# Half-size weight parts, a planner that counts the shared port of VectorE and GpSimd, packed sample rows, and values ahead of keys in a hybrid transformer step

## The chip, the cores and the metric

One core of a Trainium2 chip runs the whole program in one launch. The metric is the device time of that launch in microseconds (us). Engines are named as the profile names them: PE is TensorE (the weight loads ahead of its matmuls stand apart as PEld), DVE is VectorE, ACT is ScalarE, POOL is GpSimd, SP is SyncE, which issues nearly all DMAs.

## The reference, cut to what matters

One layer of a hybrid model, float32, for 256 prompt rows and 64 sample rows (8 requests of 8 rows). The layer has three parts side by side: sparse attention over keys that an indexer picks (A), a gated linear recurrence (B) and cross attention over a memory of 256 rows (M). Their gated outputs are joined, projected, added to the scaled input and normalized.

```python
z = jnp.einsum('btd,dn->btn', h, w)            # 2048 -> 8272 columns, 320 rows
aq, ak, av, ag, iq, ik, iw, bq, bf, bi, bg, mq, mg = jnp.split(z, cuts, axis=-1)
a_out = _dsa_prompt(aq, ak, av, iq, iw, ik)    # softmax over the top 64 keys of 256 (prompt)
...                                            # sample rows: top 256 of 2056, keys and values in cache pages
mk = jnp.einsum('bnd,dm->bnm', mem_prompt, w_mem_k[l])     # memory keys, 2048 -> 512, 256 rows
mv = jnp.einsum('bnd,dm->bnm', mem_prompt, w_mem_v[l])     # memory values, likewise
m_out = _mem_attend(mq, mk, mv)
...
cat = jnp.concatenate([a, b, m], axis=-1)
y = jnp.einsum('btn,nd->btd', cat, w_out)      # 2048 -> 2048
return _layernorm(ALPHA * h + y, ln_g, ln_b)   # rows of 2048
```

## The kernel before

**Weights.** All large products are made from two parts of each float32 operand, a rounded one (`wh`, `xh`) and the remainder (`wl`, `xl`), with three matmuls for each tile: `wh` by `xh`, `wh` by `xl`, `wl` by `xh`. Weights come in chunks of 128x1024 (512 KB) into a ring of three raw buffers `wr`. `prep` makes the parts of a chunk: ACT casts `wh<-wr`, then `wl<-wr,wh` is subtracted, on DVE for the first 52 chunks and after that (`TT`) on DVE or POOL, whichever the planner holds to be done first. `wh` and `wl` have two buffers of 128x1024 each. A raw buffer is free for the next load when its subtraction is done.

**Order.** Nothing is scheduled by the chip or a compiler: the order of each engine's instructions is what Python writes. Class `Plan` keeps a clock for each engine with estimated costs (`cost`) and latencies. The main loop of `hymba_step` goes by it: issue loads, `prep` up to one chunk ahead of the one that PE is at, evacuate finished accumulators (`pending`), let the generators of the side work go on (`background`: indexer, attention scores, softmax `soft`, recurrence `hgrn` and so on, by rank), then give PE either a unit of cached key or value pages (`unit`, `units_now`) or the next piece of a weight chunk (`pe_quantum`). Every instruction passes through one helper, so all rows have its line, L127 (L140 in the changed kernel). `T` chunks are the input projections (accumulated in `pj`), `mem` chunks the 16 of the memory keys and values (keys in two `mB` banks, values in two `pj` banks), `wo` chunks the output projection.

**A unit of pages** uses PE in another shape than the projections (`kv<-pg,qpad`, `va<-pg,PT`). `units_now` lets two follow each other, or one alone if PE has no weight piece ready.

**The output projection** runs in four column blocks n of 512; each has 8 chunks (two k tiles each), and for each chunk the row blocks m = 0, 1 (128 prompt rows each, accumulated in `mA` and `mB`, three matmuls for each k tile) and m = 2 (64 sample rows, `catS` as the weight of the array, two matmuls for each k tile, in `pj`). Of the last block, n = 3, the last `RES` = 5 chunks are kept: they are run for m = 0 alone, then all for m = 1, then all for m = 2, so that the first rows can be normalized while PE is still busy. Four of the kept chunks have their parts in memory that is spare by then (`cat0`, `cat1`, `PT`, one `pg`), the fifth in `wh` and `wl`.

**The end.** `out_chunk` adds ALPHA times the residual row to the accumulator and takes the statistics (`bn`); `finish(m)` normalizes: four pieces of 128x512, each with a DVE operation (subtract mean, times gain), an ACT scale and a POOL add of the bias. For the 64 sample rows (m = 2, in 64 of 128 partitions of a `pg` buffer) the first two pieces go that way and the other two have a second DVE operation instead of ACT and POOL. `ln_load` fetches the residual rows `xn` and the gain and bias (`lng`, `lnb`, 1 MB each).

## Time and profile before

| what | value |
|---|---|
| median of 3 runs | 922.3 us (920.91 to 923.38) |
| the profiled execution | 920.66 us |
| its span in the trace | 918.9 us, mean granted PE clock 0.991 |
| busy: PE, DVE, ACT, POOL | 884.9, 580.4, 384.6, 302.9 us |
| mean DMA rate over the span | 289 GB/s (265.53 MB) |

All rows of the trace come from the one profiled execution. It took 920.66 us, 1.76 more than its span and 1.64 less than the median. A window that shows less than its whole length as busy for PE holds waits; a wait row names the engine and the tile that ended the wait, which is the last of several that may have been late.

### The profile page before, as it was taken

The numbers are of one execution on the slowest core, as the hardware profiler recorded it, in microseconds if no ns is written. First come the engines' busy times: TensorE is split into PE (matmuls) and PEld (weight loads), VectorE is DVE, ScalarE is ACT, GpSimd is POOL, SyncE is SP. The second block draws the span as 40 slices with busy tenths as digits, with TensorE's granted clock in tenths as the row PEclk, the third lists the DMA queues.
The fourth block names the chain that finished last, engine by engine and source line by source line (L and its number), as shares of the span: only waits on it lengthen the run. The fifth ranks groups of instructions, "written<-read, shape, count | busy, mean of one in ns | idle before, by whom it ended". The sixth has DMA issues, their size and how long they took to land. (4 is left out here: it accounts for less than half of the span.)

```text
span 918.9 us, 18244 instructions
## 1 busy us (share of the span) xinstructions
PE 884.9 (96%) x6588; PEld 738.5 (80%) x6590; DVE 580.4 (63%) x1098; ACT 384.6 (42%) x677; POOL 302.9 (33%) x259
## 2 busy tenths in 40 slices
PE   8999999999999999999999999999899999999993
PEld 7999789868889987778878677778789788788872
DVE  6777995558999975757655653565354232645567
ACT  5334652544344344243443243434345232633342
POOL 0776858444644541332311311355100000011016
PEclk9999999999999999999999999999999999999997
DMA  8544435899999936999989889999994999744633
GB/s 300 176 169 151 142 100 195 334 325 359 396 367 352 386 140 220 409 383 382 367 320 401 335 304 401 404 393 337 367 336 144 409 406 381 244 144 148 202 115 114
DMA packets 79932, 265.53 MB, mean 289 GB/s; under 512 B 10081, under 2 KB 16930, under 8 KB 79266
## 3 DMA queue, kind: packets, MB, share of 16 engines
q1 hardware_dynamic: 77794, 260.17, 76.3%
q0 software_dynamic: 2048, 4.20, 1.4%
q8 instruction: 52, 0.85, 0.4%
q14 instruction: 38, 0.31, 0.1%
HBM read 255.60 MB, written 8.73 MB: 288 GB/s over the span
## 5 line engine op out<-in xcount | busy, mean ns | idle before, releaser
L127 PE MATMUL pj<-xh,wh 128*128 128x320 f32 x1008 | 324.7, 322 | 3.7 <-ACT t L127 3.7
L127 PE MATMUL pj<-xh,wl 128*128 128x320 f32 x1008 | 311.9, 309 | 1.2 <-POOL wl L127 1.1
L127 PE MATMUL pj<-xl,wh 128*128 128x320 f32 x1008 | 311.6, 309 | 0.0
L127 DVE TENSOR_TENSOR wl<-wr,wh 128x1024 fp32r<-128x1024 f32 x133 | 168.1, 1265 | 206.3 <-ACT wh L127 201.2
L127 ACT CAST wh<-wr 128x1024 fp32r<-128x1024 f32 x170 | 177.7, 1047 | 236.8 <-PE pj L127 196.1
L127 PEld LDWEIGHTS pj<-xh,wh 128*128 128x128 f32 x1008 | 189.8, 188 | 32.5 <-issue 23.5
L127 POOL TENSOR_TENSOR wl<-wr,wh 128x1024 fp32r<-128x1024 f32 x37 | 91.1, 2465 | 317.1 <-ACT wh L127 303.5
L127 PEld LDWEIGHTS pj<-xh,wl 128*128 128x128 f32 x1008 | 189.6, 188 | 1.8 <-POOL wl L127 1.3
L127 PEld LDWEIGHTS pj<-xl,wh 128*128 128x128 f32 x1008 | 190.1, 189 | 1.2
L127 POOL TENSOR_TENSOR t<-t,t 128x320 f32<-128x320 f32 (+4 forms) x74 | 68.1, 921 | 147.4 <-ACT t L127 88.9
L127 ACT ACTIVATE t<-t 128x320 f32<-128x320 f32 (+1 forms) x68 | 29.2, 454 | 77.0 <-DVE t L127 73.0
L127 PE MATMUL va<-pg,PT 128*32 128x512 f32 x512 | 60.6, 607 | 0.0
L127 PE MATMUL kv<-pg,qpad 128*32 128x256 f32 x1024 | 59.6, 381 | 0.0
L127 PEld LDWEIGHTS kv<-pg,qpad 128*32 128x32 f32 x1024 | 31.3, 110 | 23.0 <-issue 3.4
L127 POOL DMA_INDIRECT pg<-in_ci,poff x32 | 38.1, 1189 | 10.6 <-issue 8.2
L127 POOL DMA_INDIRECT S<-in_ci,poff x32 | 38.5, 1203 | 8.3 <-issue 6.6
L127 DVE MAX8 PT<-PT 128x8 f32<-128x1032 f32 x32 | 39.4, 1231 | 0.5
L127 DVE MATCH_REPLACE8 PT<-PT 128x1032 f32<-128x1032 f32 x32 | 39.0, 1218 | 0.0
L127 PEld LDWEIGHTS va<-pg,PT 128*32 128x32 f32 x512 | 14.6, 110 | 29.9 <-issue 27.2
L127 DVE TENSOR_TENSOR t<-t,t 128x128 f32<-128x128 f32 (+5 forms) x50 | 23.5, 472 | 21.0 <-ACT t L127 14.8
L127 PE MATMUL mB<-t,wh 128*128 128x256 f32 x128 | 25.8, 295 | 1.8 <-POOL t L127 1.7
L127 PE MATMUL mB<-t,t 128*128 128x64 f32 (+5 forms) x150 | 25.0, 314 | 2.2 <-POOL t L127 1.8
(309 smaller groups left out, 1280.5 us busy)
## 6 DMA issues: line engine op xcount, KB each, us to landing
pg<-in_ck SPq DMA_DIRECT2D x128, 512.0 KB
pg<-in_cv SPq DMA_DIRECT2D x128, 512.0 KB
...
```

The source lines that it names most:

```text
L127: res = f(*a, **k)
```

## The change

**Weight parts** are made in pieces of 512 columns. `prep(i, j)` casts and subtracts half a chunk; `wh` and `wl` have four buffers of 128x512; a piece of PE's work needs only its own half (`part_of`), and `prep` runs up to two chunks ahead. The 170 casts of 128x1024 become 338 of 128x512; the 133 subtractions on DVE become 246 and the 37 on POOL become 92, all of 128x512 (two small chunks at the start stay whole).

**The planner** knows a shared port: a DVE operation whose operands are all in SBUF is planned behind a POOL operation of that kind that is running. It adds 0.11 us where an operation reads what the one before it on its engine wrote, holds a change of PE's shape back to the full shape to be dearer (0.31 for 0.2), and lets a page unit run alone only if no weight piece will be ready within `SOON` = 0.4 us. `soft` gets the first rank in `background`, and waits (`need(maskb)`) before its last mask matmul.

**Prompt scores** are kept negated, so that the minimum serves as the bias of the exponential without a DVE negation; the two normalizing multiplies for each of 8 heads go from DVE to ACT.

**Memory chunks**: the values come first in the weight columns, each chunk has two pieces for PE (values, keys), and the value accumulators are evacuated (`mem_values`) apart from the keys (`mem_keys`).

**The output projection** keeps 7 chunks for n = 3 (five in spare memory), and the m = 2 pass runs in two column halves of 256, the first of which can be evacuated while the second runs.

**Sample rows** lie packed, 64 rows x 2 halves in 128 partitions of 1024 columns (`xs`, output `ys`), with a gain and bias laid out likewise (`gb`, 128x2x1024, 1 MB loaded in addition). `finish_sample` joins the statistics of the two halves by small copies between partitions and normalizes with four DVE operations of 128x512.

```diff
-RES = 5
+RES = 7
...
+        if eng != "PE" and t == self.t[eng] and not self.before[eng].isdisjoint(ki):
+            t += 0.11
+        if eng == "DVE" and port:
+            for a, b in self.port:
+                if a <= t < b - 0.1:
+                    t = b - 0.1
+        if eng == "POOL" and port:
+            self.port = self.port[-5:] + [(t, t + cost)]
+        self.before[eng] = set(ko)
...
-    for m in (1, 2):
+    for m, half in ((1, None), (2, 0), (2, 1)):
         for i in kept:
             add_wo(3, wspec[i]["k"], (m,), "main", ref=i)
+            wspec[-1]["half"] = half
...
+        w = s["n"] // s.get("parts", 2)
+        raw = WR[i][:, w * j:w * j + w]
+        if s.get("res") and kept.index(i) >= RES - 5:
             if not spare_w:
-                for cols, tag in ((2880, "cat0"), (2240, "cat1"), (2320, "PT"), (2048, "pg")):
+                for cols, tag in ((2880, "cat0"), (2240, "cat1"), (2320, "PT"), (2048, "pg"), (2048, "pg")):
                     t = new([128, cols], tag, F32R)
                     plan.split.add(t.tensor.name)
-                    spare_w.extend(t[:, 1024 * j:1024 * j + 1024] for j in range(t.shape[1] // 1024))
+                    spare_w.extend(t[:, 512 * k:512 * k + 512] for k in range(4))
             hi, lo = spare_w.pop(0), spare_w.pop(0)
...
-            hi, lo = new([128, 1024], "wh", F32R), new([128, 1024], "wl", F32R)
-        WH[i], WL[i] = whole[i] = hi, lo
-        ACT.copy(hi[:, 0:n], raw[:, 0:n])
+            hi, lo = new([128, 512], "wh", F32R), new([128, 512], "wl", F32R)
+            held["w"] += 1
+            s["held"] = True
+        WH[i].append(hi)
+        WL[i].append(lo)
+        ACT.copy(hi[:, 0:w], raw)
         if i < 52:
...
-        idle_pe = half >= len(wspec) or not half_ready(half, quarter)
-        return int(idle_pe and loaded(n) or plan.now > since[0] + PATIENCE)
+        return int(not half_soon() or plan.now > since[0] + PATIENCE)
...
-            DVE.tensor_tensor_reduce(out=P0, in0=ps[:, 0:128], in1=pbias[:, 0:128], scale=QS, scalar=FLOOR,
-                                     op0=OP.add, op1=OP.max, accum_out=s8[:, 0:1])
...
-            DVE.tensor_scalar(s8[:, 2:4], s8[:, 0:2], -1.0, None, op0=OP.mult)
+            DVE.tensor_tensor_reduce(out=P0, in0=ps[:, 0:128], in1=pbias[:, 0:128], scale=-QS, scalar=-FLOOR,
+                                     op0=OP.add, op1=OP.min, accum_out=s8[:, 0:1])
...
-            ACT.activation(P0, P0, AF.Exp, bias=s8[:, 2:3], accum_out=s8[:, 4:5])
...
+            ACT.activation(P0, P0, AF.Exp, scale=-1.0, bias=s8[:, 0:1], accum_out=s8[:, 4:5])
...
-            DVE.tensor_scalar(P0, P0, s8[:, 6:7], None, op0=OP.mult)
-            DVE.tensor_scalar(P1, P1, s8[:, 7:8], None, op0=OP.mult)
+            ACT.activation(P0, P0, AF.Copy, scale=s8[:, 6:7])
+            ACT.activation(P1, P1, AF.Copy, scale=s8[:, 7:8])
...
+        yield need(maskb)
         ps = PS([128, 8])
         PE.matmul(ps, emat[:, p % 2, 1, p // 2, :], maskb[:, 1024:1032], start=True, stop=True)
...
+            if q == 0:
+                for nt in range(2):
+                    w = slice(128 * nt, 128 * nt + 128)
+                    PE.matmul(acc[2 + nt], mh[:, w], hi, start=first, stop=False)
+                    PE.matmul(acc[2 + nt], ml[:, w], hi, start=False, stop=False)
+                    PE.matmul(acc[2 + nt], mh[:, w], lo, start=False, stop=last)
+                if last:
+                    pending.append((mem_values, acc[2:], 4))
+                return
...
             if last:
-                pending.append((mem_out, pj.pop("m"), 8))
+                pending.append((mem_keys, pj.pop("m")[0:2], 4))
...
+            st["r", 2] = r = new([128, 1024], "pg")
+            st["gb2"] = gb = new([128, 2, 1024], "pg")
+            SP.dma_start(r, I["xs"])
+            SP.dma_start(gb, I["gb"])
...
+                rows = slice(64 * (n // 2), 64 * (n // 2) + 64)
+                x = 0 if half is None else 256 * half
+                y = 512 if half is None else x + 256
+                r = st["r", 2][rows, 512 * (n % 2) + x:512 * (n % 2) + y]
+                DVE.scalar_tensor_tensor(r, r, ALPHA, ps[0:64, x:y], op0=OP.mult, op1=OP.add)
+                DVE.tensor_add(r, r, ps[64:128, x:y])
...
+        r, gb, bn, s = st["r", 2], st["gb2"], st["bns"], T8()
+        DVE.tensor_copy(bn[0:64, 4:8, :], bn[64:128, 0:4, :])
+        DVE.bn_aggr(out=s[0:64, 0:2], in_=bn[0:64])
+        ACT.activation(s[0:64, 2:3], s[0:64, 1:2], AF.Sqrt, bias=eps[0:64, 1:2])
+        DVE.tensor_copy(s[64:128, 0:1], s[0:64, 0:1])
+        for c in range(2):
+            cs = slice(512 * c, 512 * c + 512)
+            DVE.scalar_tensor_tensor(r[:, cs], r[:, cs], s[:, 0:1], gb[:, 0, cs], op0=OP.subtract, op1=OP.mult)
+            if c == 0:
+                DVE.reciprocal(s[0:64, 2:3], s[0:64, 2:3])
+                DVE.tensor_copy(s[64:128, 2:3], s[0:64, 2:3])
+        for c in range(2):
+            cs = slice(512 * c, 512 * c + 512)
+            DVE.scalar_tensor_tensor(r[:, cs], r[:, cs], s[:, 2:3], gb[:, 1, cs], op0=OP.mult, op1=OP.add)
+            SP.dma_start(O["ys"][:, cs], r[:, cs])
...
-        while nprep < nw and nprep <= half + 1 + rest_next + 2 * (half < 16) and prep_ready(nprep):
-            prep(nprep)
-            nprep += 1
+        while nprep < nw and nprep <= half + 2 + rest_next + 2 * (half < 16) and prep_ready(nprep, npart):
+            prep(nprep, npart)
+            npart += 1
```

In the order of the instructions, three places change as follows.

PE at the last memory chunk, before: `t<-…` are parts of the memory rows; the last four rows of the keys (`mB`), the six of the values (`pj`), and then the first of the next projection, which takes the `pj` buffers in turn.

```order
L127 MATMUL mB_8083<-t_9054,wl_9051 128x256
L127 MATMUL mB_8083<-t_9054,wh_9050 128x256
L127 MATMUL mB_8083<-t_9055,wh_9050 128x256
L127 MATMUL mB_8083<-t_9054,wl_9051 128x256
L127 MATMUL pj_8084<-wh_9050,t_9054 128x512
L127 MATMUL pj_8084<-wh_9050,t_9055 128x512
L127 MATMUL pj_8084<-wl_9051,t_9054 128x512
L127 MATMUL pj_8085<-wh_9050,t_9054 128x512
L127 MATMUL pj_8085<-wh_9050,t_9055 128x512
L127 MATMUL pj_8085<-wl_9051,t_9054 128x512
L127 MATMUL pj_9201<-xh,wh_9094 128x320
L127 MATMUL pj_9201<-xl,wh_9094 128x320
```

After, the values of that chunk and the first rows of its keys:

```order
L140 MATMUL pj_8579<-wl_9630,t_9633 128x512
L140 MATMUL pj_8580<-wh_9629,t_9633 128x512
L140 MATMUL pj_8580<-wh_9629,t_9634 128x512
L140 MATMUL pj_8580<-wl_9630,t_9633 128x512
L140 MATMUL mB_8577<-t_9633,wh_9637 128x256
L140 MATMUL mB_8577<-t_9634,wh_9637 128x256
L140 MATMUL mB_8577<-t_9633,wl_9638 128x256
```

and, after the other keys, a unit of key pages (`kv`) and the next projection:

```order
L140 MATMUL kv_9641<-pg_9453,qpad_368 32x256 x2
L140 MATMUL kv_9641<-pg_9525,qpad_368 32x256 x2
L140 MATMUL pj_9732<-xh,wh_9681 128x320
L140 MATMUL pj_9732<-xl,wh_9681 128x320
L140 MATMUL pj_9732<-xh,wl_9682 128x320
```

The values have moved ahead of the keys, and between the last value matmul and the next projection stand twelve matmuls of the keys and a unit of pages where nothing stood before.

DVE at the end, before: from the last normalizing operations of rows 128 to 255 (`S`) through the sample rows (`pg`).

```order
L127 SCALAR_TENSOR_TENSOR S_10503<-S_10503,s_1416_11591,pg_10768 128x512 x3
L127 SCALAR_TENSOR_TENSOR pg_10766<-pg_10766,pj_11423 64x512
L127 TENSOR_TENSOR pg_10766<-pg_10766,pj_11423 64x512
L127 BN_STATS bn_10502<-pg_10766 64x6
L127 BN_AGGR s_1417_11630<-bn_10502 64x2
L127 SCALAR_TENSOR_TENSOR pg_10766<-pg_10766,s_1417_11630,pg_10768 64x512
L127 RECIPROCAL s_1417_11630<-s_1417_11630 64x1
L127 SCALAR_TENSOR_TENSOR pg_10766<-pg_10766,s_1417_11630,pg_10768 64x512 x2
L127 SCALAR_TENSOR_TENSOR pg_10766<-pg_10766,s_1417_11630,pg_10769 64x512
L127 SCALAR_TENSOR_TENSOR pg_10766<-pg_10766,s_1417_11630,pg_10768 64x512
L127 SCALAR_TENSOR_TENSOR pg_10766<-pg_10766,s_1417_11630,pg_10769 64x512
```

After, from the second operation on the first column half of the sample rows:

```order
L140 TENSOR_TENSOR pg_11337<-pg_11337,pj_12100 64x256
L140 BN_STATS bns_11051<-pg_11337 64x6
L140 SCALAR_TENSOR_TENSOR pg_11337<-pg_11337,pj_12100 64x256
L140 TENSOR_TENSOR pg_11337<-pg_11337,pj_12100 64x256
L140 BN_STATS bns_11051<-pg_11337 64x6
L140 COPY bns_11051<-bns_11051 64x24
L140 BN_AGGR s_1756_12352<-bns_11051 64x2
L140 COPY s_1756_12352<-s_1756_12352 64x1
L140 SCALAR_TENSOR_TENSOR pg_11337<-pg_11337,s_1756_12352,pg_11338 128x512
L140 RECIPROCAL s_1756_12352<-s_1756_12352 64x1
L140 COPY s_1756_12352<-s_1756_12352 64x1
L140 SCALAR_TENSOR_TENSOR pg_11337<-pg_11337,s_1756_12352,pg_11338 128x512 x3
```

The one evacuation of 64x512 has become two of 64x256, three copies have come in, and six normalizing operations of 64x512 (with ACT's and POOL's share beside them) have become four of 128x512 on DVE alone.

POOL at the end, before: all that it does from the memory projection's last side work to the sample rows.

```order
L127 TENSOR_TENSOR t_8931<-t_8931,t_9067 128x320
L127 MEMSET bp_9298 128x1024
L127 TENSOR_TENSOR wl_11033<-wr_10962,wh_11032 128x1024
L127 TENSOR_TENSOR bp_11219<-wr_11154,bp_11218 128x1024
L127 TENSOR_TENSOR wl_11450<-wr_11385,wh_11449 128x1024
L127 TENSOR_TENSOR S_10500<-S_10500,pg_10769 128x512 x4
L127 TENSOR_TENSOR S_10503<-S_10503,pg_10769 128x512 x4
L127 TENSOR_TENSOR pg_10766<-pg_10766,pg_10769 64x512 x2
```

After, only the last rows of the same stretch:

```order
L140 TENSOR_TENSOR bp_11932<-wr_11886,bp_11931 128x512
L140 TENSOR_TENSOR bp_11970<-wr_11925,bp_11969 128x512
L140 TENSOR_TENSOR wl_12008<-wr_11963,wh_12007 128x512
L140 TENSOR_TENSOR wl_12043<-wr_11983,wh_12042 128x512
L140 TENSOR_TENSOR wl_12132<-wr_12054,wh_12131 128x512
L140 TENSOR_TENSOR cat_1746_12135<-wr_12080,cat_1746_12135 128x512 x2
L140 TENSOR_TENSOR PT_12137<-wr_12150,PT_12137 128x512
L140 TENSOR_TENSOR pg_12139<-wr_12167,pg_12139 128x512
L140 TENSOR_TENSOR S_11048<-S_11048,pg_11342 128x512 x4
L140 TENSOR_TENSOR S_11052<-S_11052,pg_11342 128x512 x4
```

Between the memory projection and the end POOL had three subtractions of 128x1024; now it has 28 of 128x512, five of them for kept chunks, and the adds for the sample rows are gone.

## Rows read from the trace of the kernel before

**Rows 1.** The page of the profile, part 1: busy time, share of the span and instructions, first of PE, then of the other engines.

```profile
PE 884.9 (96%) x6588; PEld 738.5 (80%) x6590; DVE 580.4 (63%) x1098; ACT 384.6 (42%) x677; POOL 302.9 (33%) x259
```

**Rows 2.** Windows of the span: start:end, length, then for each of PE, PEld, DVE, ACT and POOL the busy time with the number of instructions, the granted PE clock, the DMA share and GB/s.

```profile
400.00:500.00 100.00, 95.98 (x882) 80.05 (x880) 57.13 (x119) 40.94 (x73) 19.48 (x23) 1.00 0.96 365
500.00:600.00 100.00, 98.21 (x718) 75.42 (x718) 54.55 (x103) 37.84 (x66) 27.70 (x27) 0.98 0.95 365
...
884.50:892.20 7.70, 7.20 (x32) 5.46 (x31) 3.68 (x3) 4.05 (x4) 0.00 (x0) 1.00 0.36 131
892.20:899.00 6.80, 6.80 (x31) 5.60 (x30) 5.50 (x8) 3.06 (x5) 3.22 (x2) 1.00 0.00 0
...
903.70:918.90 15.20, 0.15 (x1) 0.00 (x0) 10.97 (x12) 3.03 (x5) 8.40 (x6) 0.67 0.34 106
```

**Rows 3.** Waits of PE alone, summed over the whole span: what it waited to run, for which engine's write to which tile; us in total, times, longest.

```profile
PE pj L127 <- ACT t L127: 3.7, 2, 3.0
PE mB L127 <- POOL t L127: 3.5, 3, 1.8
PE mB L127 <- DVE s L127: 2.3, 2, 2.1
PE mA L127 <- POOL t L127: 1.8, 1, 1.8
PE pj L127 <- POOL wl L127: 1.1, 1, 1.1
```

**Rows 4.** Timeline around 655 us, the end of the memory projection: start, length, engine, operation, and in brackets the idle time before it with its releaser. `t<-pj` copies the accumulators out, `pj<-xh,wh` is the next projection.

```profile
653.05 1.04 ACT L127 CAST wh<-wr 128x1024 fp32r<-128x1024 f32 x1 [2.13 <-PE pj L127]
...
655.27 0.75 DVE L127 COPY t<-pj 128x256 f32<-128x256 f32 x2
...
656.20 0.54 PE L127 MATMUL pj<-xh,wh 128*128 128x320 f32 x1 [2.96 <-ACT t L127]
```

**Rows 5.** Timeline around 466 us: a subtraction on POOL, a copy of two 128x256 tiles on DVE, and the matmul that waited for what DVE did next.

```profile
466.04 2.47 POOL L127 TENSOR_TENSOR wl<-wr,wh 128x1024 fp32r<-128x1024 f32 x1 [6.64 <-ACT wh L127]
...
466.32 2.44 DVE L127 COPY cat<-t 128x256 f32<-128x256 f32 x2
...
469.42 0.17 PE L127 MATMUL mB<-maskb,emat 128*128 128x8 bf16 x1 [2.10 <-DVE s L127]
```

**Rows 6.** Timeline around 422 us, DVE, POOL and PE: a multiply of DVE, the subtraction on POOL, and the matmul that waited in the end.

```profile
422.27 2.39 POOL L127 TENSOR_TENSOR wl<-wr,wh 128x1024 fp32r<-128x1024 f32 x1 [5.92 <-ACT wh L127]
...
422.70 2.31 DVE L127 TENSOR_TENSOR t<-t,t 128x320 f32<-128x320 f32 x1
...
426.33 0.42 DVE L127 TENSOR_TENSOR t<-t 128x256 f32<-128x256 f32 x1
...
428.36 0.32 PE L127 MATMUL mA<-t,t 128*128 128x64 f32 x1 [1.77 <-POOL t L127]
```

**Rows 7.** Timeline around 326 us: two subtractions on POOL while DVE ran operations of 128x1032, and the matmul that waited for the first of them.

```profile
325.94 7.11 POOL L127 TENSOR_TENSOR wl<-wr,wh 128x1024 fp32r<-128x1024 f32 x2 [2.14 <-ACT wh L127]
...
327.58 3.23 DVE L127 SCALAR_TENSOR_TENSOR PT<-bp,s,PT 128x1032 f32<-128x1032 f32 x1
...
329.78 0.41 PE L127 MATMUL pj<-xh,wl 128*128 128x320 f32 x1 [1.08 <-POOL wl L127]
```

**Rows 8.** Groups of instructions with shapes kept apart: operation, shapes, count | busy us, mean ns of one | idle time before. First the weight remainders as they are (128x1024), then other places' rows of 128x512.

```profile
L127 DVE TENSOR_TENSOR wl<-wr,wh 128x1024 fp32r<-128x1024 f32 x133 | 168.1, 1265 | 206.3 <-ACT wh L127 201.2 <-issue 1.8 <-PE mA L127 1.3
L127 POOL TENSOR_TENSOR wl<-wr,wh 128x1024 fp32r<-128x1024 f32 x37 | 91.1, 2465 | 317.1 <-ACT wh L127 303.5 <-DVE s L127 11.9 <-DMA pg<-in_cv 1.6
...
L127 POOL TENSOR_TENSOR S<-S,pg 128x512 f32<-128x512 f32 x8 | 11.6, 1480 | 16.5 <-ACT S L127 16.5
...
L127 DVE TENSOR_TENSOR pg<-S,qpad 128x512 fp32r<-128x512 f32 x4 | 2.8, 688 | 1.5 <-ACT qpad L127 1.5
...
L127 ACT CAST qpad<-S 128x512 fp32r<-128x512 f32 x4 | 2.5, 621 | 1.7 <-DMA S<-in_wt 1.7
```

**Rows 9.** Timeline around 785 to 797 us: the first weight cast that waits for a DMA behind the loads of the layer-norm tables.

```profile
796.83 1.05 ACT L127 CAST wh<-wr 128x1024 fp32r<-128x1024 f32 x1 [2.23 <-DMA wr<-in_wo]
```

**Rows 10.** Timeline of the first pass over the kept chunks: the issues of the last three loads (one row for the three) and the cast that each landing let start.

```profile
880.78 3.84 SPq L127 DMA_DIRECT2D wr<-in_wo  x3
...
884.12 1.05 ACT L127 CAST cat<-wr 128x1024 fp32r<-128x1024 f32 x1 [1.30 <-DMA wr<-in_wo]
...
886.60 1.05 ACT L127 CAST PT<-wr 128x1024 fp32r<-128x1024 f32 x1 [1.43 <-DMA wr<-in_wo]
...
888.76 1.05 ACT L127 CAST pg<-wr 128x1024 fp32r<-128x1024 f32 x1 [1.12 <-DMA wr<-in_wo]
```

**Rows 11.** Timeline of the end: rows 128 to 255 are `S`, the sample rows are the 64-partition `pg`.

```profile
899.24 0.69 DVE L127 SCALAR_TENSOR_TENSOR S<-S,mB 128x512 f32<-128x512 f32 x1 [1.27 <-PE mB L127]
...
903.11 5.73 POOL L127 TENSOR_TENSOR S<-S,pg 128x512 f32<-128x512 f32 x4 [1.46 <-ACT S L127]
905.19 0.67 DVE L127 SCALAR_TENSOR_TENSOR pg<-pg,pj 64x512 f32<-64x512 f32 x1
...
907.63 1.75 DVE L127 SCALAR_TENSOR_TENSOR pg<-pg,s,pg 64x512 f32<-64x512 f32 x1
...
909.38 5.50 DVE L127 SCALAR_TENSOR_TENSOR pg<-pg,s,pg 64x512 f32<-64x512 f32 x5
...
913.58 1.80 SPq L127 DMA_DIRECT2D out_y<-pg  x2
```

200 lines of the change are left out of this document (114 added, 86 removed).

## The prediction

> **What bounds the kernel now.** I read part 1 of the page first: PE is busy for 884.9 of 918.9 us, 96% [rows 1]. Side work on the other engines costs time only where PE waits for it, so a change can gain at PE's waits and at the two ends, and nowhere else. The windows show where PE is short of work: 4.02 us in 400 to 500 and 1.79 in 500 to 600, and the whole of the last 15.20 [rows 2]. The table of PE's own waits then names who was late. Its five largest entries make 12.4 us: 3.7 for copies by ACT, 3.5 + 1.8 for POOL's `t`, 2.3 for DVE's `s`, 1.1 for POOL's `wl` [rows 3]. The timelines show why. At 655 us the next projection wants a `pj` buffer, and the copy that frees it stands on ACT and DVE behind the parts of a whole chunk [rows 4]. At 466 us two copies of 128x256 take 2.44 us on DVE and end just as POOL's subtraction of 2.47 ends, and the matmul behind them waits 2.10 [rows 5]. At 422 us it is a multiply: 2.31 us, where a 128x256 one next to it takes 0.42, and PE waits 1.77 later on [rows 6]. It goes the other way as well: at 326 us two subtractions on POOL take 7.11 us together beside long DVE operations, and PE waits 1.08 for the first [rows 7].
>
> DMA is busy for 0.96 of the windows from 400 to 600, at 365 GB/s [rows 2]. Yet no entry of PE's waits names a DMA [rows 3], and the bytes stay the same; to hand over the same bytes 4 us sooner in 200, 373 GB/s would do. I don't take it for a bound.
>
> **Part 1, pieces of 512 columns.** In the form they have elsewhere, a 128x512 cast takes 0.62 us on ACT, a 128x512 subtraction 0.69 on DVE, and an elementwise POOL operation 1.48 [rows 8]. So ACT pays 338 x 0.62 = 210 us for what were 178 (1.04 each, [rows 4]); DVE 246 x 0.69 = 170 for 168.1; POOL 92 x 1.48 = 136 for 91.1. I cost that at nothing in itself: ACT stands at 384.6 us busy of 918.9 and POOL at 302.9 [rows 1], and PE hides it. If that cover fails, it does so where POOL runs beside DVE, which is the third rival. What the pieces bring: the first half is ready after 0.62 + 0.69 = 1.31 us instead of 1.04 + 1.27 = 2.31, and nothing else on ACT, DVE or POOL stands behind more than half a chunk.
>
> **Part 2, values first.** The order shows twelve key matmuls and a unit of pages between the last value matmul and the next projection. A matmul of 256 columns is half of 6.80 / 30 = 0.227 us [rows 2], so the keys alone are 1.4 us, against two copies of 0.75 together on DVE with ACT's pair beside them [rows 4]. ACT's two casts (1.24) still stand ahead of them. I leave 0.4 of the 2.96 us: **-2.6**.
>
> **Part 3, the planner and the mask.** The 2.10 us at 466 are the case for which `need(maskb)` and the first rank of `soft` are made: the matmul is no longer put into PE's queue before its input is planned to be ready. I leave 0.4: **-1.7**. POOL's `t` waits, 5.3 us [rows 3], come from DVE operations that are stretched behind a POOL subtraction as in [rows 6]. The subtraction now lasts 1.48 and not 2.47, and PE gets other work in the plan where DVE is held; somewhat over half goes: **-3.0**. Of the 1.1 us for `wl` half a chunk at a time leaves 0.3: **-0.8**. A new order has new places where the plan is wrong. I allow one wait of the size of those in [rows 6]: **+1.8**. Parts 2 and 3 together: -2.6 - 1.7 - 3.0 - 0.8 + 1.8 = -6.3. The bounds are -12.4, every entry gone and no new one, and +7 or more, below as a rival.
>
> The row at 466 us shows the wait in one direction, that at 326 us in the other; the plan delays DVE for POOL and not POOL for DVE. [...]
>
> **Part 4, negated scores.** Eight small DVE operations go and 16 multiplies move from DVE to ACT. No entry of PE's waits is for these tiles alone; nothing, and if ACT were late a few tenths.
>
> **Part 5, one more load.** `gb` adds 1 MB behind the residual rows: at 365 GB/s [rows 2] 2.9 us of DMA. The weight loads behind it come later by as much; already one cast waits 2.23 us for its DMA there [rows 9]. Five chunks are loaded ahead of that point and hide part of it. Bounds 0 and 2.9; I take **+1.0**, nearer to zero since half a chunk now starts PE.
>
> **Part 6, seven kept chunks.** The first pass takes 7.70 us [rows 2] for 30 matmuls x 0.227 = 6.8: 0.9 is lost, because the last three loads go out late, one for each raw buffer that a subtraction frees, and land 2.48 and 2.16 us apart, the last 4.26 us after the pass began [rows 10]. With seven chunks the pass has 42 x 0.227 = 9.5 us of matmuls; two more landings put the last at 4.3 + 2 x 2.3 = 8.9, its first half is ready 1.3 to 2.1 later (DVE or POOL subtracts), and 1.4 to 1.6 us of matmuls and of the second half's parts follow: 11.6 to 12.6, a loss of 2.1 to 3.1 against 0.9. POOL makes five of the remainders and frees its raw buffers late, so I take the upper end: **+2.2**. Bounds: -0.9, if two chunks of lookahead hide all loads, and +5.7, if every one of the seven is paced at 2.3 (16.1 - 9.5 - 0.9).
>
> **Part 7, the end.** Now PE stops at 903.7, and DVE's last operation ends at 909.38 + 5.50 = 914.88, 11.2 us later [rows 11]; the output and the rest of the span take another 4.0. Count from the end of the second pass, just before 899.24. DVE is taken by rows 128 to 255 until 905.19, 6.2 us [rows 11], as now. The m = 2 pass is 56 matmuls of 256 columns, 56 x 0.117 = 6.5 us (0.2 dearer than 28 x 0.227, **+0.2**), so the first half waits for DVE, not DVE for it. Two evacuations of three operations at about 0.42 (the 128x256 row in [rows 6]) bring 8.8. The copy of the statistics has both ends in SBUF, and POOL's adds run until 908.84, 9.8 after the second pass [rows 11]; I let it wait for them. Statistics, small copies and reciprocal 0.9, four operations of 128x512 at 0.7 uncontended 2.8: 13.5, with 0.2 for semaphores 13.7. That is 13.7 - 6.5 = 7.2 after PE's end, where it was 11.2: **-4.0**. Bounds -5.2 (no wait for POOL, 0.69 each) and -2.0 (the four at 1.1 us, as the five in a row of 5.50 are now [rows 11]).
>
> The sample rows now leave from 128 partitions, before from 64. [...]
>
> **Sum.** Parts 2 and 3 -6.3, parts 1 and 4 nothing, then +1.0 + 2.2 + 0.2 - 4.0: -6.9. Against the profiled execution's 920.66 us that is 913.8. That execution is 1.64 below the median of 922.3; I don't add this, since the waits of a plan made for less contention may well shrink more than I allow.
>
> **Rivals.** (a) **The waits move.** POOL's pieces wait behind DVE's long operations as at 326 us [rows 7], and new waits eat what part 3 gains; only values-first and the end count: -2.6 + 1.0 + 2.2 + 0.2 - 4.0 = -3.2, 917.5. For it: the plan delays one side alone. Against: half-length pieces. (b) **No change:** as (a), and the first pass is paced by all seven loads: -3.2 + 3.5 = +0.3, 921.0. For it: landings 2.3 us apart against 1.4 of matmuls for a chunk. Against: lookahead of two chunks. (c) **Slower: POOL's 92 pieces each cost PE what the 37 did.** POOL-made waits are 3.5 + 1.8 + 1.1 + 2.3 = 8.7 us [rows 3], 0.235 for each subtraction. At 92 that is 21.6, +12.9, and with the other terms of -3.2 it gives +9.7, 930.4. It ends slower by over 0.3% from 0.16 us a piece on. For it: the number of chances to collide. Against: a piece that lasts 0.6 as long, and a plan that sees DVE's side. (d) **More gain:** all five entries go and the first pass keeps its loss of now: -12.4 + 1.0 + 0.2 - 4.0 = -15.2, 905.5.
>
> **Chances.** A measurement of this kernel tells about 0.3%, 2.8 us, from no change. Forecast (907 to 917) 0.55, (d) 0.12, (a) 0.12, (b) 0.11, (c) 0.10. Faster 0.79, same 0.11, slower 0.10. The range takes in (d), (a) and (b) and leaves (c) out: 905 to 921.5.
>
> **What the profile after would show.** PE's waits for `t` by ACT under 1 us and for `s` by DVE near zero; POOL's `wl` row x92 near 1.5 us; the first pass of n = 3 about 12 us for 42 matmuls; from PE's last matmul to the end about 11 us. The prediction is wrong if PE's waits add up to what they did under new names, if casts before the kept chunks wait for DMA by several us, or if `wl` pieces on POOL come out at 2 us or more.

## The result, and the profile after

The changed kernel takes 907.81 us (906.29 to 910.70), beside 922.41 for the kernel before on the same chip: ratio 0.9847 [0.9817, 0.9877], 14.6 us less. Faster was forecast, by 6.9; the time lies in the range, near the lower end of the forecast's own 907 to 917, and nearer to rival (d), 905.5, than to the forecast, 913.8. The profiled execution took 908.86 us (span 907.1, mean granted PE clock 0.998, before 0.991). Between the two profiled executions the difference is 11.8 us, and that is the one taken apart here.

Part 1 of the page, after ([rows 1] before):

```profile
PE 882.3 (97%) x6615; PEld 738.2 (81%) x6618; DVE 580.8 (64%) x1198; ACT 414.7 (46%) x872; POOL 324.5 (36%) x315
```

PE is busy 2.6 us less, and of the span it is not busy for 907.1 - 882.3 = 24.8 us, where it was 918.9 - 884.9 = 34.0. These two make the 11.8. Windows show in which stage. After (start:end, length, busy time of PE, PEld, DVE, ACT and POOL with instructions, granted clock, DMA share, GB/s):

```profile
0.00:100.00 100.00, 93.25 (x622) 85.89 (x623) 74.70 (x178) 47.76 (x90) 51.53 (x59) 1.00 0.62 192
100.00:200.00 100.00, 96.81 (x659) 79.39 (x658) 79.93 (x180) 59.07 (x120) 49.49 (x53) 1.00 0.56 185
...
400.00:500.00 100.00, 99.84 (x917) 81.81 (x917) 62.92 (x142) 44.45 (x91) 33.64 (x35) 1.00 0.99 380
500.00:600.00 100.00, 100.00 (x778) 79.82 (x778) 54.72 (x130) 42.72 (x90) 33.37 (x38) 1.00 1.00 381
...
867.57:881.10 13.53, 11.86 (x43) 7.22 (x42) 8.92 (x14) 7.38 (x12) 6.38 (x5) 1.00 0.43 133
...
897.20:907.10 9.90, 0.24 (x3) 0.03 (x1) 6.26 (x15) 0.39 (x2) 2.92 (x3) 0.77 0.40 159
```

And stretches of the kernel before that the prediction had not looked at, the last two with a granted clock of about half:

```profile
0.00:100.00 100.00, 96.52 (x640) 88.47 (x641) 73.28 (x164) 47.32 (x73) 54.86 (x59) 1.00 0.56 194
100.00:200.00 100.00, 98.41 (x668) 82.35 (x670) 69.35 (x137) 50.47 (x83) 63.78 (x60) 1.00 0.61 215
...
510.00:513.00 3.00, 3.00 (x16) 1.01 (x9) 1.94 (x4) 0.96 (x2) 0.84 (x2) 0.50 0.42 164
...
656.00:660.00 4.00, 3.80 (x15) 3.80 (x16) 0.68 (x3) 1.08 (x4) 0.00 (x0) 0.57 1.03 413
```

Time in which PE is not busy, by stage, from such windows:

| stage, us | before | after | difference |
|---|---|---|---|
| 0 to 200 | 5.1 | 9.9 | +4.9 |
| 200 to 300 | 0.3 | 0.0 | -0.3 |
| 300 to 700 | 12.7 | 3.5 | -9.2 |
| 700 to 860 | 0.4 | 0.0 | -0.4 |
| 860 to the end | 15.5 | 11.3 | -4.2 |
| sum | 34.0 | 24.8 | -9.2 |

Two stages give 13.4 us and one takes 4.9 back. Of the 2.6 us by which PE is less busy, the clock is the largest part: before, it stood at half for 3.0 us at 510 and at 0.57 for 4.0 us at 656, which loses 3.0 x 0.50 + 4.0 x 0.43 = 3.2 us; after, it is 1.00 in each window of 100 us from 300 to 700. The first pass over the kept chunks goes the other way: it is 13.53 us long for 42 matmuls that would fill 42 x 0.227 = 9.5, and is recorded as busy for 11.86.

PE's waits, after (for which engine's write to which tile; us in total, times, longest):

```profile
PE mA L140 <- POOL t L140: 2.8, 2, 2.1
PE mA L140 <- DVE cat L140: 1.5, 2, 1.0
...
PE pj L140 <- POOL wl L140: 0.9, 1, 0.9
...
PE pj L140 <- ACT t L140: 0.6, 1, 0.6
```

Against [rows 3], ACT's `t` is down from 3.7 to 0.6, and what is left is a wait at 22 us that the kernel before has too (0.69); the 2.96 us are gone. DVE's `s` is gone. The 2.8 us for POOL's `t` is not what is left of the old 5.3: both waits lie before 100 us, where the kernel before had none of that name. From 300 to 700, POOL's `t` is gone. New in this stretch is a mask matmul that waits 1.11 us for ACT's `t` at 652, and POOL's `wl` costs 0.85 at 676 where it cost 1.08 at 330. Summed over all names, the table of PE's waits has 18.5 us before and 15.1 after.

The weight remainders, after ([rows 8] before):

```profile
L140 DVE TENSOR_TENSOR wl<-wr,wh 128x512 fp32r<-128x512 f32 x246 | 191.1, 787 | 211.1 <-ACT wh L140 197.8 <-PE pj L140 6.1 <-issue 4.9
L140 POOL TENSOR_TENSOR wl<-wr,wh 128x512 fp32r<-128x512 f32 x92 | 123.0, 1342 | 325.0 <-ACT wh L140 316.9 <-DMA wr<-in_wo 6.4 <-PE va L140 1.5
```

POOL's piece takes 1.34 us (forecast 1.48), DVE's 0.79 (forecast 0.69). DVE pays 21 us more than was worked out from the undisturbed row, and POOL 13 less.

The end, after, DVE's timeline (start, length, operation, and in brackets the idle time before it; [rows 11] before):

```profile
893.43 3.10 DVE L140 SCALAR_TENSOR_TENSOR S<-S,s,pg 128x512 f32<-128x512 f32 x3
897.48 0.42 DVE L140 SCALAR_TENSOR_TENSOR pg<-pg,pj 64x256 f32<-64x256 f32 x1 [0.95 <-PE pj L140]
...
900.19 0.17 DVE L140 COPY bns<-bns 64x24 f32<-64x24 f32 x1
...
900.98 0.75 DVE L140 SCALAR_TENSOR_TENSOR pg<-pg,s,pg 128x512 f32<-128x512 f32 x1
...
902.01 2.08 DVE L140 SCALAR_TENSOR_TENSOR pg<-pg,s,pg 128x512 f32<-128x512 f32 x3
```

PE ends at 897.2 and DVE at 904.09, 6.9 later (forecast 7.2, before 11.2). But DVE is idle for 0.95 us and starts on the first column half only after PE's last matmul.

The first pass, after, the casts of ACT that waited for their loads ([rows 10] before):

```profile
873.30 1.14 ACT L140 CAST PT<-wr 128x512 fp32r<-128x512 f32 x2 [3.06 <-DMA wr<-in_wo]
876.24 1.14 ACT L140 CAST pg<-wr 128x512 fp32r<-128x512 f32 x2 [1.80 <-DMA wr<-in_wo]
878.06 1.14 ACT L140 CAST pg<-wr 128x512 fp32r<-128x512 f32 x2 [0.68 <-DMA wr<-in_wo]
```

### The profile page after: what moved, and what is told of

It is laid out like the page before. It is cut to its first block, busy times and chain, and to the rows that moved or that the text cites. A ratio compares the mean times of both kernels' runs of the same rounds, so it can differ in the third digit from the quotient of the medians.

```text
span 907.1 us, 18917 instructions
## 1 busy us (share of the span) xinstructions
PE 882.3 (97%) x6615; PEld 738.2 (81%) x6618; DVE 580.8 (64%) x1198; ACT 414.7 (46%) x872; POOL 324.5 (36%) x315
## 4 chain that ended last, share of the span: by engine, by line
PE 75%; DVE 8%; ACT 1%; DMA 1%; issue 1%; POOL 0%; DVEq 0%; ACTq 0%
PE pj L140 41%; PE mB L140 11%; PE mA L140 9%; PE va L140 8%; PE kv L140 6%; DVE PT L140 4%; DVE t L140 1%; DVE pg L140 1%; ACT wh L140 1%; DMA wr<-in_wo 1%; DVE cat L140 0%; DVE s L140 0%; DVE wl L140 0%; DVE bp L140 0%; DMA S<-in_ci,poff 0%
## 5 line engine op out<-in xcount | busy, mean ns | idle before, releaser
L140 DVE TENSOR_TENSOR wl<-wr,wh 128x512 fp32r<-128x512 f32 x246 | 191.1, 787 | 211.1 <-ACT wh L140 197.8
L140 ACT CAST wh<-wr 128x512 fp32r<-128x512 f32 x338 | 204.0, 618 | 211.1 <-PE pj L140 164.2
L140 POOL TENSOR_TENSOR wl<-wr,wh 128x512 fp32r<-128x512 f32 x92 | 123.0, 1342 | 325.0 <-ACT wh L140 316.9
L140 POOL TENSOR_TENSOR t<-t,t 128x256 fp32r<-128x256 f32 (+4 forms) x69 | 55.7, 808 | 125.7 <-ACT t L140 79.1
L140 PE MATMUL va<-pg,PT 128*32 128x512 f32 x512 | 58.7, 596 | 0.0
L140 PEld LDWEIGHTS va<-pg,PT 128*32 128x32 f32 x512 | 14.8, 109 | 30.8 <-issue 28.7
L140 POOL DMA_INDIRECT pg<-in_ci,poff x32 | 34.4, 1074 | 11.8 <-issue 8.8
L140 POOL DMA_INDIRECT S<-in_ci,poff x32 | 33.9, 1060 | 9.0 <-issue 8.5
L140 DVE TENSOR_TENSOR t<-t,t 128x320 f32<-128x320 f32 (+4 forms) x55 | 23.0, 418 | 21.9 <-ACT t L140 15.7
L140 POOL TENSOR_TENSOR t<-t,tabm 128x320 f32<-128x320 f32 x16 | 14.0, 876 | 43.7 <-DVE t L140 38.4
L140 PE MATMUL mA<-t,t 128*128 128x64 f32 (+6 forms) x172 | 26.3, 300 | 2.8 <-POOL t L140 2.8
```

What stands on the lines that cost most here:

```text
L140: res = f(*a, **k)
```

## The experiments

My first theory was the prediction's sum with larger terms: the planner and the values-first order remove the waits, the end gives 5, and the pieces only change who does how much. The rivals to it: the pieces themselves bring the gain and the planner little; or the planner costs. Each expectation says what its theories give for that run. Runs marked "old planner" keep `need(maskb)` and the first rank of `soft`, and put the plan's costs and rules back as they were. Times are medians, and the kernel before has 922.4 to 923.1 beside all of them.

**keys_first**: the changed kernel with the keys as first piece and the values as second.

```diff
-            if q == 0:
+            if q == 1:
                 for nt in range(2):
...
-                    pending.append((mem_values, acc[2:], 4))
+                    pending.append((mem_values, pj.pop("m")[2:], 4))
```

> The changed kernel with one part undone: in each memory chunk the keys come first again and the values second, as two pieces. Theory 1 (the order within the last chunk is what removed the wait at 653 us): the next projection waits again for the value accumulators, about 1.5 to 3 us for ACT's t, and PE runs at half clock for about 3.3 us after it, which costs another 1.5: 3 to 4.5 us slower than the changed kernel. Rival (the half-size pieces alone had shortened the evacuation's queue enough): no wait over 1 us there, within 1.5 us of the changed kernel.

905.36 us (904.19 to 906.08), ratio 0.9815 [0.9785, 0.9845]. The wait comes back: the copies stand behind two casts on ACT and a subtraction on DVE, each of half a chunk.

```profile
643.47 1.13 ACT L140 CAST wh<-wr 128x512 fp32r<-128x512 f32 x2
644.11 0.69 DVE L140 TENSOR_TENSOR wl<-wr,wh 128x512 fp32r<-128x512 f32 x1 [3.19 <-ACT wh L140]
644.72 0.75 DVE L140 COPY t<-pj 128x256 f32<-128x256 f32 x2
645.23 0.65 ACT L140 COPY t<-pj 128x256 f32<-128x256 f32 x2 [0.63 <-DVE t L140]
645.65 0.42 PE L140 MATMUL pj<-xh,wh 128*128 128x320 f32 x1 [2.77 <-ACT t L140]
```

Yet the kernel is not slower, since it loses less elsewhere: in its first 200 us PE is not busy for 4.6 us, in the changed kernel for 9.9, though the instructions there are in the same order (below, on the start). That half-size pieces do not remove this wait by themselves is shown; what values-first is worth is not, by this run.

**mem_only**: the kernel before with the values first, as a PE piece of their own, and nothing else.

```diff
+            if q == 0:
+                for nt in range(2):
+                    w = slice(128 * nt, 128 * nt + 128)
+                    PE.matmul(acc[2 + nt], mh[:, w], hi[:, 512:1024], start=first, stop=False)
...
+                if last:
+                    pending.append((mem_values, acc[2:], 4))
+                return
```

> The kernel before with one part alone: in each memory chunk the values first, evacuated apart from the keys; weight parts stay 1024 wide. Theory 1: the wait of 2.96 us at 656 us goes and with it the stretch of half clock behind it (656.3 to 659.6, matmuls 0.265 us apart where 0.146 is usual, 1.5 us lost): 4 to 4.5 us faster than before. Rival (the copies still stand behind the parts of a whole chunk): the wait stays above 1.5 us, and the gain is under 2 us.

921.07 us, ratio 0.9984 [0.9970, 0.9999]: 1.4 less, within 0.3%; between the profiled executions it is 0.2. PE's waits, and a window:

```profile
PE pj L127 <- POOL t L127: 2.8, 4, 1.0
...
PE pj L127 <- ACT t L127: 1.7, 2, 1.0
```

```profile
429.00:433.00 4.00, 4.00 (x39) 2.44 (x28) 2.67 (x8) 2.32 (x5) 1.54 (x3) 0.57 1.03 410
```

ACT's `t` falls from 3.7 to 1.7 ([rows 3]); the wait of 2.96 and the half clock behind it are gone. In their place the value matmuls, which now come first in each chunk, wait four times for POOL's parts of the memory rows and once for ACT's, 3.9 us in all; before, two key matmuls waited for such parts, 1.7 us. So PE's idle time from 300 to 700 us falls by only 0.8. And the clock gives nothing: the stretch at 656 is gone, but the one above is new. It follows a wait of 1.77 us that the kernel before has as well (428.36, [rows 6]), at full clock there (1.00 from 428 to 433).

**port_off**: the changed kernel without the rule that delays DVE behind POOL.

```diff
-        if eng == "DVE" and port:
-            for a, b in self.port:
-                if a <= t < b - 0.1:
-                    t = b - 0.1
```

> The changed kernel without the rule that plans a DVE operation behind a running POOL operation; everything else stays. Theory 1 (the plan's order round DVE and POOL is what removed the waits of 1.8 to 2.1 us at 426, 466 and 506): such waits come back, 3 to 6 us slower than the changed kernel. Rival (a POOL subtraction of 1.34 instead of 2.47 us did it by its length): within 1.5 us of the changed kernel, no wait over 1.5 us between 300 and 700 us.

913.49 us, ratio 0.9897 [0.9866, 0.9928]: 5.7 more than with the rule. Timeline around 323 us, DVE and then PE:

```profile
324.41 1.64 DVE L136 TENSOR_SCALAR maskb<-PT 128x1032 bf16<-128x1032 f32 x1
...
326.10 0.38 PE L136 MATMUL mB<-maskb,emat 128*128 128x512 bf16 x1 [2.33 <-DVE maskb L136]
```

and the windows behind that wait and a second one at 654:

```profile
326.00:330.00 4.00, 3.85 (x43) 2.63 (x44) 2.76 (x10) 1.47 (x4) 1.28 (x1) 0.59 0.63 177
...
657.00:661.00 4.00, 4.00 (x19) 4.00 (x18) 0.41 (x4) 2.66 (x3) 0.75 (x1) 0.60 1.02 405
```

Behind each of these waits of over 2 us about 1.6 us (4.0 x 0.41, 4.0 x 0.40) are lost at the lower clock; a third one, 2.33 at 631.86, is followed by full clock. The rule pays, and where it works it pays more than 5.7: from 300 to 700 us PE is not busy for 11.1 us here and for 3.5 with the rule, while the first 200 us, for another reason (last section), hold 5.4 here and 9.9 with it.

**plan_old**: the changed kernel with all of the old planner.

```diff
-            t += 0.11
...
-                turn = 0.31 if shape == (128, 128) else 0.09 if self.shape == (128, 128) else 0.2
+                turn = 0.2 if shape == (128, 128) else 0.09 if self.shape == (128, 128) else 0.2
...
-        return int(not half_soon() or plan.now > since[0] + PATIENCE)
+        idle_pe = half >= len(wspec) or not half_ready(half, quarter)
+        return int(idle_pe and loaded(n) or plan.now > since[0] + PATIENCE)
```

(The lines of the port rule go too, and a constant in the cost of one kind of operation goes back to +0.12 from -0.05.)

> The changed kernel with the whole old planner: no shared port, no 0.11 us for a read right after a write, the old price of a change of PE's shape and of the max operations, and a lone page unit only when PE has nothing ready. Pieces of 512, values first, seven kept chunks and packed sample rows stay. Theory 1 (the plan counts for about half of the 5 to 6 us gained between 300 and 700 us): 3 to 6 us slower than the changed kernel. Rival (the pieces did it): within 1.5 us. The waits that are new in the changed kernel before 200 us (5 us more than before) should go if they come from the new plan.

902.12 us (902.02 to 902.36), ratio 0.9777 [0.9747, 0.9806]: 5.7 less than the changed kernel, 5.0 less than its second run below. The new planner as a whole costs, although one of its rules pays. PE is not busy for 4.0 us of the first 200, as the expectation said if those waits came from the new plan; but keys_first, with the new plan, has 4.6 there, so they need not. This overthrew the first theory, so the next runs took the pieces by themselves.

**after_again**: the changed kernel once more, beside the next three on one chip.

> The changed kernel itself again, to stand beside the next kernels on one chip and to show how far its own executions differ. Theory 1 (its first result, 906.3 to 910.7, holds 2.4 to 4 us of waits before 100 us that come and go between executions of one program): a profile whose waits before 100 us are 3 us or more below the 8 us of the first, and a median of 905 to 907. Rival (these waits belong to the order): the same waits at 44, 62 and 79 us, median 907 to 909.

907.10 us, ratio 0.9844 [0.9813, 0.9874]. PE's three waits for POOL's `t` before 100 us are there again, at 44, 61 and 78 us. They are 0.72, 0.72 and 0.67 long, where they were 2.12, 0.78 and 0.66: the places belong to the program, the lengths vary between executions, and PE is not busy there for 5.0 us instead of 6.7. Neither theory held whole.

**whole** and **whole_old**: the changed kernel with parts of a whole chunk (128x1024) again, with the new and with the old planner.

```diff
-        w = s["n"] // s.get("parts", 2)
+        w = s["n"]
...
-            hi, lo = new([128, 512], "wh", F32R), new([128, 512], "wl", F32R)
+            hi, lo = new([128, 1024], "wh", F32R), new([128, 1024], "wl", F32R)
...
-        return q * wspec[i].get("parts", 2) // wspec[i]["nq"]
+        return 0
```

> The changed kernel with one part undone: weight parts of 1024 columns in two buffers each, made a whole chunk at a time; the new planner, values first, seven kept chunks and packed rows stay. Theory 1 (the pieces, not the planner, removed the waits between 300 and 700 us): 4 to 7 us slower than the changed kernel, waits of over 1.5 us and one or two stretches of half clock come back. Rival (the planner did): within 2 us.

> Both undone: weight parts of 1024 columns and the old planner; seven kept chunks, packed rows, values first, negated scores and the earlier mask softmax stay. Theory 1 (pieces are worth the same under either planner, and the old planner is the better one): 4 to 7 us slower than pieces with the old planner (902.1), so 906 to 909, and faster than whole parts with the new planner. Rival (the two need each other): 912 or more, most of the gain of the pieces gone with the planner.

919.97 us, ratio 0.9968 [0.9952, 0.9985], and 916.90, ratio 0.9929 [0.9913, 0.9946]. With the pieces it is 907.10 and 902.12: whichever planner there is, they are worth 12.9 and 14.8 us, and whichever size, the new planner costs 3.1 and 5.0 (0.4 and 2.6 of these in the first 100 us, by the busy time of PE). PE's waits in the first of the two:

```profile
PE pj L140 <- POOL wl L140: 3.5, 1, 3.5
PE mB L140 <- ACT t L140: 2.3, 1, 2.3
PE mA L140 <- POOL wl L140: 2.2, 2, 1.5
```

POOL's `wl`, 0.9 us with pieces, makes 5.7 when a remainder on POOL is a whole chunk.

Not all of this is waiting. In the profiled executions, **whole** has four stretches at about half clock (at 131, 326, 606 and 660 us), each of which loses 1.7 us by its windows; **whole_old** has one (328), and the changed kernel and plan_old have none before the end. So of the pieces' 14.8 us between the profiled executions of whole and after_again 7.6 are idle time of PE and 6.8 clock, and of the 15.6 between whole_old and plan_old 11.2 are idle time and 1.7 clock. With whole parts PE is idle as long under either planner (30.5 and 30.2 us), so the planner's 3.1 us there need be no more than those stretches.

**rows64**: the changed kernel with the sample rows in 64 partitions, as before, and without `gb`.

```diff
-            DVE.scalar_tensor_tensor(r[:, cs], r[:, cs], s[:, 0:1], g[:, cs], op0=OP.subtract, op1=OP.mult)
+            DVE.scalar_tensor_tensor(r[:, cs], r[:, cs], s[:, 0:1], g[0:rows, cs], op0=OP.subtract, op1=OP.mult)
...
+            if m < 2 or c < 2:
+                ACT.activation(r[:, cs], r[:, cs], AF.Copy, scale=s[:, 2:3])
+                POOL.tensor_add(r[:, cs], r[:, cs], b[0:rows, cs])
+            else:
+                DVE.scalar_tensor_tensor(r[:, cs], r[:, cs], s[:, 2:3], b[0:rows, cs], op0=OP.mult, op1=OP.add)
```

> The changed kernel with the sample rows in 64 partitions of 2048 columns again, without the added table load; the m = 2 pass stays in two halves, seven chunks stay kept. Theory 1 (the packing carries the end): from PE's last matmul to the end 12.5 to 13.5 us where the changed kernel has 9.9, so 2.5 to 3.5 us slower. Rival (the end is mostly shortened by the longer cover of rows 128 to 255): under 1.5 us slower. The added load of 1 MB costs PE nothing if the stretch from 700 to 860 us has the same waits in both.

915.90 us, ratio 0.9914 [0.9891, 0.9936], 8.8 more than after_again. The end shows 3.6 of it, 13.5 us from PE's last matmul instead of 9.9, with the five normalizing operations in a row that [rows 11] have:

```profile
900.60:914.10 13.50, 0.24 (x3) 0.03 (x1) 9.04 (x14) 1.75 (x4) 6.18 (x5) 0.60 0.38 117
```

Most of the rest lies in the first 100 us, where nothing was edited: PE is not busy there for 7.6 us, in after_again for 5.0, and from 46 to 50 us it runs at a clock of 0.57, another 1.7 lost. So only the end counts for the rows. From 700 to 860 us PE is never idle in either, so the load of `gb` costs nothing.

**pieces_only**: the kernel before with pieces, four half-size buffers for two whole ones and the longer lookahead: planner, rank of `soft`, keys before values, five kept chunks and the end are those of before. Each memory chunk has two pieces for PE here too (keys, then values).

```diff
-    BUFS = {"t": 16, "s8": 10, "pg": 6, "bp": 2, "wr": 3, "wh": 2, "wl": 2, "S": 2, "mA": 2, "mB": 2, "pj": 2}
+    BUFS = {"t": 16, "s8": 10, "pg": 6, "bp": 2, "wr": 3, "wh": 4, "wl": 4, "S": 2, "mA": 2, "mB": 2, "pj": 2}
...
+        w = s["n"] // s.get("parts", 2)
+        raw = WR[i][:, w * j:w * j + w]
...
+            hi, lo = new([128, 512], "wh", F32R), new([128, 512], "wl", F32R)
```

> The kernel before with one part alone: weight parts in pieces of 512 columns, prepared up to two chunks ahead, with the old planner, keys first, five kept chunks, sample rows in 64 partitions and positive scores. Theory 1 (the pieces carry most of the change; with everything else they made 12.9 us under the new planner and 14.8 under the old): 9 to 14 us faster than before, 908 to 913, and the waits at 426, 466 and 506 us and the half clock gone. Rival (they pay only together with the other parts): less than 6 us faster, 916 or more.

908.30 us, ratio 0.9854 [0.9826, 0.9882]: 14.2 less than the kernel before, as much as the whole change brings. Part 1 of its page, and PE's waits:

```profile
PE 882.2 (97%) x6590; PEld 737.2 (81%) x6590; DVE 594.9 (66%) x1219; ACT 413.4 (46%) x859; POOL 326.3 (36%) x316
```

```profile
PE mA L134 <- DVE t L134: 2.8, 3, 1.5
...
PE pj L134 <- ACT t L134: 0.6, 1, 0.6
...
PE mB L134 <- DVE s L134: 0.3, 1, 0.3
```

With a span of 906.6, PE is not busy for 24.4 us, and 14.9 of them are the end, as long as before (15.0). The other stages hold 9.5, where they held 34.0 - 15.0 = 19.0. No wait for POOL's `t` or POOL's `wl` is in its table, DVE's `s` is down from 2.3 to 0.3, and ACT's `t` is at 0.6, the wait at 22 us, though the values still come last and the mask has no new `need`. No stretch of half clock is left before the end. So this edit alone removes nearly all that the five entries of [rows 3] held from 300 to 700 us.

How it does so is not always by a shorter part ahead. At the end of the memory projection nothing stands ahead of the copies:

```profile
642.89 0.42 DVE L134 COPY t<-pj 128x256 f32<-128x256 f32 x1 [0.27 <-PE pj L134]
...
644.28 1.14 ACT L134 CAST wh<-wr 128x512 fp32r<-128x512 f32 x2
...
644.65 0.41 PE L134 MATMUL pj<-xh,wh 128*128 128x320 f32 x1
```

They wait for PE alone, the casts come after them, and PE has a unit of key pages of 1.93 us to do meanwhile. In keys_first, with pieces of the same size, the copies stand behind the parts and PE waits 2.77. Here it is the order that the planner makes of the pieces that removes the wait.

**old_port**: plan_old plus the port rule.

```diff
+        if eng == "DVE" and port:
+            for a, b in self.port:
+                if a <= t < b - 0.1:
+                    t = b - 0.1
```

> Pieces and all other parts of the change, with the old planner and the rule on the shared port alone added to it. Theory 1 (the rule makes the order better in itself; without it the new planner was 6 us slower): 2 us or more faster than the old planner without it (902.1), so 900 or less. Rival (it only mends what the other new rules of the planner break): 901 to 906.

899.07 us (898.52 to 899.22), ratio 0.9749 [0.9725, 0.9774], the fastest of all: 8.7 below the changed kernel, 3.0 below plan_old. So the port rule pays 3.0 here and 5.7 in the new planner, and the planner's other rules together cost 907.10 - 899.07 = 8.0 with it and 913.49 - 902.12 = 11.4 without it (port_off against plan_old, neither of which has the waits at the start). Of the 8.0, 2.1 lie in the first 100 us (PE is busy there for 97.06, in after_again for 94.99), where, as the last section shows, the order need not be the cause; about 6 are left for the rules.

**old_res5**: plan_old with five kept chunks.

```diff
-RES = 7
+RES = 5
```

> All parts of the change with the old planner, but five kept chunks, as before, and not seven. Theory 1 (what the longer cover saves at the end, the first pass gives back waiting for loads): the first pass loses about 2 us less, from PE's last matmul to the end about 2 us more, within 1 us of 902.1. Rival (seven chunks carry the end): 2 us or more slower, 904 or more.

900.61 us (899.35 to 902.33), ratio 0.9769 [0.9741, 0.9798], 1.5 less than with seven. From PE's last matmul to the end it takes 12.0 us, since the tail now meets POOL's adds:

```profile
891.31 0.87 DVE L134 COPY bns<-bns 64x24 f32<-64x24 f32 x1
```

This copy waits for the adds on POOL, which run until 892.15; it takes 0.17 in the changed kernel. Still the whole is shorter, and the first pass shows why; first here, then in plan_old:

```profile
868.60:875.50 6.90, 6.90 (x32) 5.65 (x31) 1.99 (x3) 3.57 (x5) 2.11 (x2) 1.00 0.29 115
```

```profile
861.19:874.66 13.47, 11.19 (x43) 7.51 (x42) 8.94 (x14) 7.39 (x12) 6.43 (x5) 1.00 0.42 134
```

Five chunks lose 0.1 us against 30 x 0.227 = 6.8, seven lose 3.9 against 9.5. The two extra kept chunks cost 3.8 us more there and give 2.1 at the end (12.0 to 9.9).

**old_banks**: plan_old with an accumulator of its own for each column half.

```diff
+                    if n == 3:
+                        pj[key][2] = [pj[key][2], PS([128, 512], "kv")]
...
+                    PE.matmul(o[2][j][:, 0:256], catS[:, K, :], hi[:, c], start=first, stop=False)
+                    PE.matmul(o[2][j][:, 0:256], catS[:, K, :], lo[:, c], start=False, stop=stop)
```

> All parts of the change with the old planner, and the two column halves of the m = 2 pass in accumulators of their own (a bank of pj and the bank of kv), where the changed kernel has both in one; two matmuls more for each k tile of the first chunk of n = 3. In the changed kernel the first half's evacuation waited for the last matmul of the second, 0.95 us of idle DVE. Theory 1 (one tile, one wait): the first half is now evacuated while the second runs, 0.8 to 1.2 us faster than 902.1. Rival (DVE is busy with rows 128 to 255 for so long that it does not matter): within 0.4 us.

901.89 us (901.75 to 905.08), ratio 0.9793 [0.9763, 0.9824], the same as plan_old. Timeline of its end, DVE:

```profile
889.74 0.42 DVE L134 SCALAR_TENSOR_TENSOR pg<-pg,pj 64x256 f32<-64x256 f32 x1
...
892.47 0.86 DVE L134 COPY bns<-bns 64x24 f32<-64x24 f32 x1
```

and POOL:

```profile
887.54 5.76 POOL L134 TENSOR_TENSOR S<-S,pg 128x512 f32<-128x512 f32 x4 [3.79 <-ACT S L134]
```

The first half no longer waits for PE (no bracket at 889.74; 0.95 in the changed kernel). The copy then starts at 892.47 and takes 0.86 instead of 0.17, because POOL's adds last until 893.30. The wait moved from PE to POOL.

## Why the prediction was right, and where not

The sign and the range held, and so did three of the mechanisms: values-first removes its wait, planning DVE behind POOL pays, and four operations of 2.8 us close the end. The sum was too small by 7.7 us of the medians (by 4.9 of the profiled executions), and the gain was credited to the wrong parts. That the time lies in the range is luck in good part: a term put at nothing measured 13 to 15 us, the planner's gain was a loss, and waits at the start and in the first pass took back part of what the pieces gave beyond the forecast.

| term of the prediction | forecast | measured |
|---|---|---|
| part 1, pieces | 0 | -12.9 and -14.8 in the changed kernel, -14.2 alone |
| part 2, values first | -2.6 | -1.4 alone (profiled executions: -0.2) |
| part 3, planner and mask | -3.7 | planner +3.1 and +5.0; mask not tried by itself |
| parts 2 and 3, waits, 300 to 700 us | -6.3 | -9.2 (PE not busy), clock -3.2 beside it |
| part 5, `gb` | +1.0 | no loss: 700 to 860 has no idle time, with it or without (rows64) |
| part 6, first pass | +2.2 | +3.1 |
| part 7, the end | -4.0 | -5.3 |

**Part 1 is the step that failed.** I worked out the sums of busy time for the pieces and, since PE hides them, put "nothing in itself". Those sums were roughly right (ACT 204 us for 210, DVE 191 for 170, POOL 123 for 136) and without weight. I had a gain in words as well ("nothing else on ACT, DVE or POOL stands behind more than half a chunk") without giving it a price. pieces_only shows the price, 14.2 us: with values last, no `need(maskb)` and the old planner it removes the waits that I had credited to those three. Which part of the edit does it was not run apart: the shorter operations, the buffers that come free by halves (the cast that the copies stood behind in [rows 4] came late itself, after 2.13 us of waiting for PE), the longer lookahead, or the second PE piece in each memory chunk. The words that I had are not the whole of it: at the memory projection the copies ran behind no part at all.

**Part 2.** The mechanism is as described: the 2.96 us vanish when the values come first (mem_only) and 2.77 come back when they don't (keys_first). The price was wrong, because the value matmuls, now first in each chunk, wait for the parts of the memory rows longer than the keys did (3.9 us for 1.7, mem_only); this is what rival (a) says, in this one place. With pieces it hangs on the planner: pieces_only has no wait there with the values last, keys_first has 2.77.

**Part 3.** "The plan delays DVE for POOL" is worth 3.0 to 5.7 us (old_port, port_off). That the two share a port is the planner's model; what the traces show is operations that last longer beside each other (a copy of 0.87 us on DVE that ends with POOL's adds in old_res5, 0.17 after them in the changed kernel; two subtractions of 7.11 together on POOL, [rows 7], where the mean of one is 2.47, [rows 8]). POOL's `wl`, forecast at -0.8, went from 1.1 to 0.9. The rest of the planner I had not costed at all, only the new wait of 1.8; it costs 6 to 11. Which of its rules does (0.11 for reading what was just written, the dearer change of shape, the constant, `SOON`) wasn't tried apart.

**The new waits** that I allowed 1.8 us for: 1.11 us came in the middle (at 652), and +4.9 in the first 200 us. The latter are not shown to be a matter of the order: keys_first has the same order there and 4.6 us, less than the kernel before with 5.1; see the last section.

**Part 6** came out beyond its own upper end: 13.53 us for 9.5 of matmuls is a loss of 4.0, where 3.1 had been the most for the forecast (the bound of the rival was 5.7 more). The seventh chunk's parts lay behind loads that came 2.94 and 1.82 us apart. On balance two more kept chunks cost about 1.7 us by the stages and 1.5 by the medians (old_res5).

**Part 7** was right in what it ends with (four operations 0.75 + 2.08 = 2.83, forecast 2.8) and wrong on the way. "The first half waits for DVE, not DVE for it" does not hold: both halves lie in one accumulator tile, and DVE waited 0.95 us for the second half's last matmul before it took the first. And the copy that I let wait for POOL came just after the adds (894.35 + 5.77 = 900.12, the copy at 900.19). The two errors nearly cancel, and old_banks shows that they belong together. The remaining 1.0 us is the output: 904.09 to 907.1 is 3.0 us, before 4.0. rows64, with these rows in 64 partitions as before, has 3.9 (904.71 + 5.50 = 910.21 to 914.1); what of the 1.0 belongs to the partitions is not shown, since the difference holds other things as well.

**Rivals.** (c) did not come: 92 pieces on POOL make 0.9 us of PE's waits for `wl`, not 0.235 each. (d) gave the nearest time, and in part for its reason, since four of the five entries go from 300 to 700 (`wl` keeps 0.85); but the first pass did not keep its loss, and the clock and the start, which it does not speak of, nearly cancel.

**The signs of being wrong.** The first came most of the way: PE's waits add up to 15.1 us under new names, after 18.5. The second came too: the casts before the kept chunks wait 4.9 us for DMA, 2.5 before (longest 3.2 and 2.2), though PE is not idle there. The third did not: a piece on POOL takes 1.34 us.

**What stays open.** Which part of the pieces' edit brings the 14 us, and which planner rule costs the 6 to 11. What old_port, five chunks and separate accumulators give together: it wasn't run. What makes the waits at the start. Of the 2.6 us by which PE is less busy, 3.2 (clock) and 0.2 (the halves of the m = 2 pass) and some 1.9 (the first pass, 11.86 - 9.5 against 7.20 - 6.8) leave about -1.5 that I can't place.
